# A second load of the second down-projection chunk, and later transposes, in a one-core decoder block

## The chip, the core and the metric

The kernel runs on one core of a Trainium2 chip. A core has five engines with queues of their own: TensorE (PE in the profile: matmuls and transposes; PEld is its loading of weights), VectorE (DVE), ScalarE (ACT), GpSimd (POOL) and SyncE (SP). SP and POOL also issue transfers between the chip's memory and the core's buffer, which 16 DMA engines carry out; those issued by SP show as queue q1 in the profile, those by POOL as q0. The metric is the time of one execution on the device, in microseconds (us). Lower is better.

## The reference

One layer of a decoder block, 512 tokens of 1024 features, in 32-bit floats:

```python
h = rmsnorm(x, pre_mix_norm[l])
proj = h @ w_in[l]                      # queries, keys, values, gates of both mixers
ret = silu(g_r) * retention_chunkwise(q_r, k_r, v_r)
y_r, y_s = ret @ w_ret_out[l], swa @ w_swa_out[l]
merged = sigmoid(gate_r) * y_r + sigmoid(gate_s) * y_s
x = x + rmsnorm(merged @ w_out[l], post_mix_norm[l])
h = rmsnorm(x, pre_mlp_norm[l])
u = jnp.square(jax.nn.relu(h @ w_up[l]))        # 1024 -> 4096
x = x + rmsnorm(u @ w_down[l], post_mlp_norm[l])   # 4096 -> 1024
```

The change concerns the last three lines: the normalised h (h2 in the kernel), the up projection and the down projection.

## The kernel before

**Precision.** Each 32-bit operand is split into a high part, rounded by a copy on ScalarE (`split`, L145), and the low rest, a subtraction on VectorE (L147). A product is three matmuls on TensorE (`mm3`, L190 to L192): high by high, high by low, low by high. whi and wlo are the parts of a weight chunk, left those of the activations. They live in rings: four buffers each for whi and wlo, two for left.

**Fewer products.** Large projections use a Winograd form of the 2 x 2 block product: seven block products instead of eight, with sums of blocks of the weights and of the activations as operands. Sums of weight blocks are made by the transfers: SP loads one block, and POOL issues a second transfer that adds another block into the same buffer (`t_add`, L1296, for w_down; L223 for w_up). Such a transfer is called an add below.

**Up projection.** h2 is transposed on TensorE in two halves of the tokens (`transpose_h2`: four groups of four 128 x 128 transposes into a PSUM bank tin, L1173, each evicted by ScalarE and VectorE). The first NH = 3 blocks of 256 features are computed the plain way by `up_half` (a bank named up, 8 times 3 matmuls of 256 columns), first for the first half of the tokens, so that TensorE has work while the second half is normalised. The transposes of the second half stand after the two blocks fp = 0 and 1, then come the third block and the second half. Blocks 3 to 15 run in Winograd form (`up_pair`, banks named wino); results, squared after relu, go to uc0 to uc3.

**Down projection.** w_down comes in chunks of 1 MB: [128, 4, 512] for a block product and one of four groups j of the 4096 features. tch0 to tch3 hold chunk j of the sum operand T: loaded with block (0, 0), used by p1(j), then an add of block (0, 1) makes the operand of p5(j), two more adds make those of p6(j) and p4(j). The chunks of p2(j) come through raw, a ring of two buffers that is shared with the weight loads of all stages before; rb[j], for p3 and p7, use raw too but for one, which has a buffer of its own. Each product of one j (`product2`) is 24 matmuls of 512 columns, and each needs two halves of whi, of wlo, and one left. The order is

```python
for step, j in ((step_p1, 0), (step_p2, 0), (step_p1, 1), (step_p5, 0), (step_p2, 1),
                (step_p1, 2), (step_p5, 1), (step_p2, 2), (step_p1, 3), (step_p5, 2),
```

tch0 has memory that is free during the up projection. tch1 to tch3 and g_out lie in a pool (dpool3) that takes the memory which the up projection's pools give back, so their loads wait for the last wino matmul that reads from there.

**What sets the order.** A scheduler lays each engine's instructions in one list before the run: by the order of the program, moved ahead by `tc.high_priority(offset)`, held back by `tc.issue_after(ins)`, which places what the block issues on the engine of ins behind ins without a wait for its end, and by what is ready first in its own estimate. At run time each engine takes its list strictly in turn. A transfer is issued when its buffer is free (the last reader of what lay there has finished) and, for an add, when what it adds to has landed and been read.

Of the kernel before, what the change touches and what calls it, by code (L numbers as in the profile page):

```python
# [16 lines left out]
P = 128  # L17
# [14 lines left out]
CHAIN_AHEAD = 400  # L32
SUMS_AHEAD = 0
# [71 lines left out]
def block_kernel(ctx, tc, x, xT, pre_mix, w_in, w_qk, w_v, w_g, w_gate, w_ret, w_swa, w_out, sinks, post_mix,  # L105
                 pre_mlp, w_up, w_down, post_mlp, decay, chunk, dist, out):
    nc = tc.nc
# [8 lines left out]
    def bank(shape, name="ps"):  # L116
        return psum.tile(shape, F32, tag="ps", name=name)
# [23 lines left out]
    last = {}  # L141

    def split(hi, lo, src):

        last["hi"] = nc.scalar.copy(hi, src)  # L145
        last["prior"] = last.get("split")
        last["split"] = nc.vector.tensor_tensor(lo, src, f(hi), op=ALU.subtract)  # L147

    def raw_tile(shape):
        return stream.tile(shape, F32, name="raw", tag="raw", bufs=2)  # L150

    def parts(src, shape):
        hi = stream.tile(shape, F32R, name="whi", tag="whi")
        lo = stream.tile(shape, F32R, name="wlo", tag="wlo")
        split(hi, lo, src)
        return hi, lo
# [30 lines left out]
    def mm3(ps, a, b, first, last, more=False):  # L187

        (ah, al), (bh, bl) = a, b
        nc.tensor.matmul(ps, ah, bh, start=first, stop=False, skip_group_check=more)  # L190
        nc.tensor.matmul(ps, ah, bl, start=False, stop=False, skip_group_check=more)  # L191
        nc.tensor.matmul(ps, al, bh, start=False, stop=last, skip_group_check=more)  # L192

# [1 line left out]
    def wino_pool(stack, side="left"):  # L197
        return stack.enter_context(tc.tile_pool(name="wx", bufs=1, side=side))

    def wino_tokens(wx, b11, b12, b21, b22, f, dst):  # L200

        f11, f12, f21, f22 = f
        nc.vector.tensor_tensor(f11, f11, f12, op=ALU.subtract)
        split(dst[0][:, 0], dst[1][:, 0], f11)
        nc.vector.tensor_tensor(f12, f22, f12, op=ALU.subtract)
        split(dst[0][:, 2], dst[1][:, 2], f12)

        nc.vector.scalar_tensor_tensor(f22, f22, -1.0, f11, op0=ALU.mult, op1=ALU.subtract)
        split(dst[0][:, 1], dst[1][:, 1], f22)
        nc.vector.scalar_tensor_tensor(f21, f22, -1.0, f21, op0=ALU.mult, op1=ALU.subtract)  # L210
        split(dst[0][:, 3], dst[1][:, 3], f21)
        sums = [tuple(d[:, i] for d in dst) for i in range(4)]
        return {"11": b11, "21": b21, "22": b22, "t1": sums[0], "t2": sums[1],
                "t3": sums[2], "t4": sums[3]}
# [50 lines left out]
    def wino_product(ps, a, b, first=True):  # L265
        for k in range(4):
            mm3(
                ps, tuple(o[:, k] for o in a), tuple(o[:, k] for o in b),
                first and k == 0, k == 3, not first,
            )  # L270

    def entry(ps, left, right):

        nc.tensor.matmul(ps, f(left), f(right), start=True, stop=True)
# [106 lines left out]
    for k in range(KD):  # L381
        split(wkv[0][:, k], wkv[1][:, k], raw_kv[:, k])
        split_scaled(xg[0][:, k], xg[1][:, k], xTs[:, k], gT[:, k : k + 1])
        for t in range(NT):
            mm3(kv_ps[t], xcol(k, t), tuple(a[:, k] for a in wkv), k == 0, k == KD - 1)
# [369 lines left out]
    for g in range(SWA_KV):  # L755
        ps = bank([P, SEQ])
# [93 lines left out]
    for h in range(RET_HEADS):  # L850
# [29 lines left out]
        if h == 0:  # L880
# [4 lines left out]
            wx = wino_pool(gctx)  # L885
# [208 lines left out]
    for half in range(2):  # L1094
        zs = [[None, None], [None, None]]
        for n in range(2):
            for t in range(2):
                tt = 2 * half + t
                ps = bank([P, 512])
# [24 lines left out]
    NH = 3  # L1124
# [12 lines left out]
    h2s = [h2spool.tile([P, 4, 4, 256], F32R, name=f"h2s{i}") for i in range(2)]  # L1137
# [3 lines left out]
    wx = wino_pool(uctx)  # L1141
# [4 lines left out]
    quads = [  # L1146
        [tuple(a[:, 0] for a in h2c), tuple(h2b)],
        [tuple(a[:, 1] for a in h2c), tuple(h2d)],
    ]
    h2f = [[uc[3][:, 2 * i + j] for j in range(2)] for i in range(2)]  # L1150

    def up_half(fp, b, w, half):
        both = bank([P, 2, 256], "up")
        ps = both[:, 0]
        if (fp, b, half) == (0, 0, 0):
            entry(both[:, 1, :ENTRY], w[0][:, 0], quads[0][0][0][:, 0, :ENTRY])
        for k in range(KD):
            kw = (k + 4) % KD if b else k
            mm3(
                ps, (w[0][:, kw, :], w[1][:, kw, :]),  # L1160
                tuple(a[:, k % 4] for a in quads[k // 4][half]), k == 0, k == KD - 1,
            )
        dst = uc[fp // 4][:, 2 * b + half, fp % 4]
        nc.scalar.activation(dst, ps, AF.Relu)
        nc.scalar.activation(dst, dst, AF.Square)

    def transpose_h2(half):
        for kp in range(KD // 2):
            ps = bank([P, 2, 256], "tin")
            for k in range(2):  # L1170
                kk = 2 * kp + k
                for t in range(2):
                    nc.tensor.transpose(  # L1173
                        ps[:, k, t * P : (t + 1) * P],
                        h2[2 * half + t][:, kk * P : (kk + 1) * P], ident,
                    )
            i, k0 = kp // 2, 2 * (kp % 2)
            hi, lo = quads[i][half]
            if half and kp == KD // 2 - 1:
                rows = h2[2 * half + 1][:, kk * P : (kk + 1) * P]  # L1180
                entry(bank([P, ENTRY], "entry"), rows, quads[0][0][0][:, 0, :ENTRY])
            split(hi[:, k0 : k0 + 2], lo[:, k0 : k0 + 2], ps)
            nc.scalar.copy(h2f[i][half][:, k0 : k0 + 2], ps)

    held = {}

    def load_up_pair(fp):
        raw = raw_tile([P, 4, 4, P])
        nc.sync.dma_start(raw, w_up[fp])
        return [  # L1190
            parts(raw[:, q : q + 2].rearrange("p q k c -> p (q k) c"), [P, KD, P]) for q in (2, 0)
        ]

    def first_ups(half, fps):
        for fp in fps:
            if half == 0 or fp == 0:
                held[fp] = load_up_pair(fp)
            for b in range(2):
                up_half(fp, b, held[fp][b], half)

    with tc.high_priority(offset=H2_AHEAD):
        transpose_h2(0)
    first_ups(0, range(NH - 1))
    with tc.high_priority(offset=CHAIN_AHEAD):
        transpose_h2(1)
    with tc.high_priority(offset=SUMS_AHEAD):
        h2B = wino_tokens(
            wx, quads[0][0], quads[0][1], quads[1][0], quads[1][1],
            [h2f[0][0], h2f[0][1], h2f[1][0], h2f[1][1]], h2s,
        )  # L1210
    first_ups(0, (NH - 1,))
    first_ups(1, range(NH)[::-1])
    pctx.close()
    tctx.close()
# [5 lines left out]
    tch = [None] * 4  # L1220
# [54 lines left out]
    def left(j, q):  # L1275
        hi, lo = (ring.tile([P, 4, 256], F32R, name=f"left{i}") for i in range(2))
        split(hi, lo, uc[j][:, q])
        return hi, lo

    def right(src):  # L1280
        return [parts(src[:, 2 * i : 2 * i + 2], [P, 2, 512]) for i in range(2)]
# [8 lines left out]
    def product2(ps, j, a, b):  # L1290
        for h in range(2):
            for tb in range(2):
                product(ps, a, b, h, j == 0, j == 3, tb)

    def t_add(dst, k, c, j):
        nc.gpsimd.dma_start(dst, w_down[k, c, j], accum_op=ALU.add)  # L1296

    def load_b(k, c, j, alone=2):
        raw = stream2.tile([P, 4, 512], F32, name="rb") if j == alone else raw_tile([P, 4, 512])
        nc.sync.dma_start(raw, w_down[k, c, j])  # L1300
        return raw
# [8 lines left out]
    p1, p2, p5 = banks2("p1"), banks2("p2"), banks2("p5")  # L1310

    def step_p1(j):
        with tc.high_priority(offset=LEFT_AHEAD if j == 0 else 0):
            with tc.issue_after(last["chain2"].ins):
                b = [parts(tch[j][:, :2], [P, 2, 512])] if j == 0 else right(tch[j])
            with tc.issue_after(last["chain"].ins):
                a = left(j, 0)
            if j == 0:
                with tc.issue_after(last["hi"].ins), tc.issue_after(last["split"].ins):
                    b.append(parts(tch[j][:, 2:], [P, 2, 512]))  # L1320
        t_add(tch[j], 0, 1, j)
        product2(p1, j, a, b)

# [14 lines left out]
    for step, j in ((step_p1, 0), (step_p2, 0), (step_p1, 1), (step_p5, 0), (step_p2, 1),  # L1338
                    (step_p1, 2), (step_p5, 1), (step_p2, 2), (step_p1, 3), (step_p5, 2),
                    (step_p2, 3), (step_p5, 3)):  # L1340
        step(j)
# [85 lines left out]
    for j in range(2):  # L1427
        a, b = left(j, 3), right(tch[j])
# [21 lines left out]
    for i in range(2):  # L1450
        c = slice(i * 256, (i + 1) * 256)
        ps = bank([P, 256], "p4c")
# [53 lines left out]
```

## Time and profile before

| | |
|---|---|
| runs | 718.5, 718.7, 720.9 us; median 718.7 |
| profiled execution | 718.92 us, span of its profile 717.1 us, granted TensorE clock 0.997 |
| TensorE matmul busy | 705.3 us, 98% of the span |
| VectorE, ScalarE, GpSimd busy | 539.3, 430.7, 61.3 us |
| bytes moved by transfers | 119.37 MB, mean 166 GB/s |

Times in rows are counted from the start of the span. A timeline row gives start, duration, engine, line, operation, the tile written and those read, and in brackets the idle time just before it with what ended it. A waits row gives the waiting engine and line, what it waited for, the us in total, the times, and the longest. A row on transfers gives the tiles, the issuing queue, the size, and the us from issue to landing. A busy TensorE share is of pipelined matmuls: each lasts longer than the distance to the next one.

### The profile page before, as it was taken

The numbers are of one execution on the slowest core, as the hardware profiler recorded it, in microseconds if no ns is written. First come the engines' busy times: TensorE is split into PE (matmuls) and PEld (weight loads), VectorE is DVE, ScalarE is ACT, GpSimd is POOL, SyncE is SP. The second block draws the span as 40 slices with busy tenths as digits, with TensorE's granted clock in tenths as the row PEclk, the third lists the DMA queues.
The fourth block names the chain that finished last, engine by engine and source line by source line (L and its number), as shares of the span: only waits on it lengthen the run. The fifth ranks groups of instructions, "written<-read, shape, count | busy, mean of one in ns | idle before, by whom it ended". The sixth has DMA issues, their size and how long they took to land.

```text
span 717.1 us, 11473 instructions
## 1 busy us (share of the span) xinstructions
PE 705.3 (98%) x4528; PEld 630.1 (88%) x4528; DVE 539.3 (75%) x816; ACT 430.7 (60%) x733; POOL 61.3 (9%) x77
## 2 busy tenths in 40 slices
PE   9999999999999999999999999999999999999996
PEld 8877879898788999989888999999999788888885
DVE  5699988685985767566945866778777688977797
ACT  6657667566665525435733866766668566655561
POOL 0200100121100000000011100000000110010010
PEclk9999999999999999999999999999999999999998
DMA  9964623966444455553661619876753999698603
GB/s 316 333 176 89 151 60 102 266 154 139 89 148 117 129 137 147 156 168 101 218 258 69 162 45 283 205 192 158 212 144 118 315 273 237 148 207 198 117 1 117
DMA packets 40613, 119.37 MB, mean 166 GB/s; under 512 B 3568, under 2 KB 17008, under 8 KB 34416
## 3 DMA queue, kind: packets, MB, share of 16 engines
q1 hardware_dynamic: 33504, 81.28, 32.4%
q0 software_dynamic: 6768, 37.23, 27.8%
q8 instruction: 35, 0.57, 0.3%
q14 instruction: 18, 0.15, 0.1%
q10 hardware_dynamic: 288, 0.14, 0.1%
HBM read 116.54 MB, written 2.10 MB: 165 GB/s over the span
## 4 chain that ended last, share of the span: by engine, by line
PE 76%; DVE 9%; DMA 7%; ACT 5%; issue 2%; POOL 1%; POOLq 0%; SPq 0%; DVEq 0%; ACTq 0%
PE wino L190 9%; PE wino L192 9%; PE wino L191 9%; PE p L191 5%; PE p L190 5%; PE p L192 5%; DVE wlo L147 3%; DMA raw<-in_w_in 3%; PE yr L192 2%; PE yr L190 2%; PE ps L190 2%; PE ps L192 2%; PE yr L191 2%; PE ps L191 2%; ACT whi L145 2%
## 5 line engine op out<-in xcount | busy, mean ns | idle before, releaser
L147 DVE TENSOR_TENSOR wlo<-raw,whi 128x1024 fp32r<-128x1024 f32 (+1 forms) x80 | 96.3, 1208 | 41.2 <-ACT whi L145 41.1
L145 ACT CAST whi<-raw 128x1024 fp32r<-128x1024 f32 (+1 forms) x80 | 82.9, 1042 | 32.6 <-DMA raw<-in_w_in 7.2
L191 PE MATMUL p<-wlo,left 128*128 128x512 f32 x216 | 84.2, 390 | 0.8 <-DVE wlo L147 0.8
L190 PE MATMUL p<-whi,left 128*128 128x512 f32 x216 | 84.1, 390 | 0.6 <-ACT whi L145 0.6
L192 PE MATMUL p<-whi,left 128*128 128x512 f32 x216 | 84.0, 390 | 0.0
L190 PEld LDWEIGHTS p<-whi,left 128*128 128x128 f32 x216 | 40.5, 188 | 9.7 <-ACT whi L145 1.0
L191 PEld LDWEIGHTS p<-wlo,left 128*128 128x128 f32 x216 | 40.5, 188 | 9.5 <-DVE wlo L147 1.1
L192 PEld LDWEIGHTS p<-whi,left 128*128 128x128 f32 x216 | 40.5, 188 | 8.7 <-DVE left L147 0.4
L147 DVE TENSOR_TENSOR wlo<-tch,whi 128x1024 fp32r<-128x1024 f32 x32 | 38.7, 1219 | 9.2 <-ACT whi L145 9.2
L145 ACT CAST p<-rs 128x1024 fp32r<-128x1024 f32 x22 | 23.1, 1052 | 36.5 <-DVE rs L244 36.4
L145 ACT CAST left<-uc 128x1024 fp32r<-128x1024 f32 x28 | 29.4, 1052 | 23.1 <-PE p L191 19.8
L147 DVE TENSOR_TENSOR left<-uc,left 128x1024 fp32r<-128x1024 f32 x28 | 34.1, 1220 | 10.2 <-ACT left L145 10.2
L145 ACT CAST whi<-tch 128x1024 fp32r<-128x1024 f32 x32 | 33.3, 1049 | 13.6 <-PE p L192 6.5
L147 DVE TENSOR_TENSOR p<-rs,p 128x1024 fp32r<-128x1024 f32 x22 | 27.0, 1226 | 16.7 <-ACT p L145 16.7
L147 DVE TENSOR_TENSOR wlo<-rs,whi 128x1024 fp32r<-128x1024 f32 x23 | 28.1, 1224 | 15.1 <-ACT whi L145 12.5
L190 PE MATMUL wino<-h2s,p 128*128 128x256 f32 x104 | 28.8, 277 | 0.0
L192 PE MATMUL wino<-h2s,p 128*128 128x256 f32 x104 | 28.7, 276 | 0.0
L191 PE MATMUL wino<-h2s,p 128*128 128x256 f32 x104 | 28.7, 276 | 0.0
L190 PE MATMUL wino<-h2c,whi 128*128 128x256 f32 x104 | 28.7, 276 | 0.0
L191 PE MATMUL wino<-h2c,whi 128*128 128x256 f32 x104 | 28.7, 276 | 0.0
L192 PE MATMUL wino<-h2c,wlo 128*128 128x256 f32 x104 | 28.7, 276 | 0.0
L190 PE MATMUL wino<-h2s,whi 128*128 128x256 f32 x104 | 28.7, 276 | 0.0
(411 smaller groups left out, 2352.2 us busy)
## 6 DMA issues: line engine op xcount, KB each, us to landing
tch<-in_w_down POOLq DMA_DIRECT2D x12, 1024.0 KB, 9.2
raw<-in_w_down SPq DMA_DIRECT2D x7, 1024.0 KB, 7.8
rs<-in_w_up SPq DMA_DIRECT2D x13, 512.0 KB, 4.5
rs<-in_w_up POOLq DMA_DIRECT2D x13, 512.0 KB, 5.6
raw<-in_w_up SPq DMA_DIRECT2D x13, 512.0 KB, 5.4
acc<-in_w_v POOLq DMA_DIRECT2D x4, 1024.0 KB, 9.0
rs<-in_w_gate SPq DMA_DIRECT2D x8, 512.0 KB, 4.1
acc<-in_w_g POOLq DMA_DIRECT2D x4, 1024.0 KB, 8.0
```

The lines of the kernel that those rows point to most:

```text
L145: last["hi"] = nc.scalar.copy(hi, src)
L147: last["split"] = nc.vector.tensor_tensor(lo, src, f(hi), op=ALU.subtract)
L190: nc.tensor.matmul(ps, ah, bh, start=first, stop=False, skip_group_check=more)
L191: nc.tensor.matmul(ps, ah, bl, start=False, stop=False, skip_group_check=more)
L192: nc.tensor.matmul(ps, al, bh, start=False, stop=last, skip_group_check=more)
```

## The change

It has two parts. In the first, `step_p1(1)` no longer reads tch1 but a second copy of the same chunk, loaded into a raw buffer (`load_b(0, 0, 1, 4)`); tch1 is loaded as before and serves from the add for p5(1) on. In the second, `transpose_h2(1)` and the sums behind it are issued from within `up_half` of the block fp = 1, b = 1: behind the sixth of its 24 matmuls (k = 1), by `tc.issue_after`. mm3 returns its last matmul for that.

```diff
-    def up_half(fp, b, w, half):
+    def up_half(fp, b, w, half, amid=None):
...
-            mm3(
+            done = mm3(
                 ps, (w[0][:, kw, :], w[1][:, kw, :]),
                 tuple(a[:, k % 4] for a in quads[k // 4][half]), k == 0, k == KD - 1,
             )
+            if amid and k == 1:
+                amid(done.ins)
...
-                up_half(fp, b, held[fp][b], half)
+                up_half(fp, b, held[fp][b], half, amid if b and fp == NH - 2 else None)
...
-    first_ups(0, range(NH - 1))
-    with tc.high_priority(offset=CHAIN_AHEAD):
-        transpose_h2(1)
-    with tc.high_priority(offset=SUMS_AHEAD):
-        h2B = wino_tokens(
-            wx, quads[0][0], quads[0][1], quads[1][0], quads[1][1],
-            [h2f[0][0], h2f[0][1], h2f[1][0], h2f[1][1]], h2s,
-        )
+    h2B = {}
+
+    def second_half(ins):
+        with tc.high_priority(offset=CHAIN_AHEAD), tc.issue_after(ins):
+            transpose_h2(1)
+        with tc.high_priority(offset=SUMS_AHEAD):
+            h2B.update(wino_tokens(
+                wx, quads[0][0], quads[0][1], quads[1][0], quads[1][1],
+                [h2f[0][0], h2f[0][1], h2f[1][0], h2f[1][1]], h2s,
+            ))
+
+    first_ups(0, range(NH - 1), second_half)
...
     def step_p1(j):
+        src = load_b(0, 0, j, 4) if j == 1 else tch[j]
         with tc.high_priority(offset=LEFT_AHEAD if j == 0 else 0):
             with tc.issue_after(last["chain2"].ins):
-                b = [parts(tch[j][:, :2], [P, 2, 512])] if j == 0 else right(tch[j])
+                b = [parts(src[:, :2], [P, 2, 512])] if j == 0 else right(src)
```

SP's list around the start of the down projection, before. raw_6240 is for p2(0), raw_6354 for p2(1), raw_6468 for p2(2); rb_6871 is for p3(2).

```order
L1300 DMA raw_6240<-in_w_down 128x2048
L1300 DMA raw_6354<-in_w_down 128x2048
L1225 DMA tch1_6166<-in_w_down 128x2048
L1225 DMA tch2_6168<-in_w_down 128x2048
L1225 DMA tch3_6170<-in_w_down 128x2048
L1267 DMA g_out_6172<-in_post_mlp_norm 128x1024
L1300 DMA raw_6468<-in_w_down 128x2048
L1300 DMA rb_6871<-in_w_down 128x2048
```

And with the change, where raw_6274 is the second copy for p1(1), raw_6356 is for p2(1) and raw_6470 for p2(2):

```order
L1306 DMA raw_6240<-in_w_down 128x2048
L1306 DMA raw_6274<-in_w_down 128x2048
L1231 DMA tch1_6166<-in_w_down 128x2048
L1231 DMA tch2_6168<-in_w_down 128x2048
L1231 DMA tch3_6170<-in_w_down 128x2048
L1273 DMA g_out_6172<-in_post_mlp_norm 128x1024
L1306 DMA raw_6356<-in_w_down 128x2048
L1306 DMA raw_6470<-in_w_down 128x2048
L1306 DMA rb_6873<-in_w_down 128x2048
```

The copy for p1(1) took the second place, and the load for p2(1) moved from there to behind the three tch loads and g_out.

POOL's list of adds, before, with the semaphores that each waits for (DVE: an instruction of VectorE; DMAHW: a load issued by SP; DMASW: an add; PE: a matmul):

```order
L1296 DMA tch0_4566<-in_w_down 128x2048 [waits DVE_49]
L1296 DMA tch1_6166<-in_w_down 128x2048 [waits DMAHW6_49,DVE_49]
L1296 DMA tch0_4566<-in_w_down 128x2048 [waits DMASW7_49,DVE_49]
L1296 DMA tch2_6168<-in_w_down 128x2048 [waits DMAHW7_49,DVE_49]
L1296 DMA tch1_6166<-in_w_down 128x2048 [waits DMASW0_49,DVE_49]
```

With the change:

```order
L1302 DMA tch0_4566<-in_w_down 128x2048 [waits DVE_49]
L1302 DMA tch1_6166<-in_w_down 128x2048 [waits DMAHW6_49,PE_49]
L1302 DMA tch0_4566<-in_w_down 128x2048 [waits DMASW7_49,DVE_49]
L1302 DMA tch2_6168<-in_w_down 128x2048 [waits DMAHW7_49,DVE_49]
L1302 DMA tch1_6166<-in_w_down 128x2048 [waits DMASW0_49,DVE_49]
```

The first add into tch1 no longer waits for VectorE, which read tch1 for p1(1), but for the load into tch1 and for the matmul that the load into tch1 itself waits for, the last wino matmul on that memory.

TensorE's list at the transposes of the second half, as the difference (with its sign) between the two:

```order
 L190 MATMUL up<-h2c_4095,whi 128x256
-L1173 MATMUL tin<-ident,zg 128x128 x16
+L191 MATMUL up<-h2c_4096,whi 128x256
+L192 MATMUL up<-h2c_4095,wlo 128x256
+L190 MATMUL up<-h2c_4095,whi 128x256
+L191 MATMUL up<-h2c_4096,whi 128x256
+L192 MATMUL up<-h2c_4095,wlo 128x256
+L1175 MATMUL tin<-ident,zg 128x128 x16
 L274 MATMUL entry<-h2c_4095,zg 128x32
```

The sixteen transposes moved behind five matmuls of the block fp = 1 that stood after them; the one ahead of them was there before. All other matmuls keep their places.

More of the change, by code (lines that the diff above doesn't have):

```diff
@@ L191, in mm3 @@
         nc.tensor.matmul(ps, ah, bl, start=False, stop=False, skip_group_check=more)
-        nc.tensor.matmul(ps, al, bh, start=False, stop=last, skip_group_check=more)
+        return nc.tensor.matmul(ps, al, bh, start=False, stop=last, skip_group_check=more)
     def wino_pool(stack, side="left"):
@@ L1192, in load_up_pair, with first_ups @@
         ]
-    def first_ups(half, fps):
+    def first_ups(half, fps, amid=None):
         for fp in fps:
@@ L1319, in step_p1 @@
                 with tc.issue_after(last["hi"].ins), tc.issue_after(last["split"].ins):
-                    b.append(parts(tch[j][:, 2:], [P, 2, 512]))
+                    b.append(parts(src[:, 2:], [P, 2, 512]))
         t_add(tch[j], 0, 1, j)
```

## The prediction

> **What bounds the kernel now.** I read the page first, for the engine that is full.
>
> ```profile
> span 717.1 us, 11473 instructions
> PE 705.3 (98%) x4528; PEld 630.1 (88%) x4528; DVE 539.3 (75%) x816; ACT 430.7 (60%) x733; POOL 61.3 (9%) x77
> ```
>
> TensorE is busy 98% of the span. An edit that leaves its matmuls alone can win only the time in which TensorE stands, and every new stand is a loss. The view of waits, for TensorE alone, gives the stands (us in total, times, longest); three of its rows belong to this change:
>
> ```profile
> PE p L191 <- DVE wlo L147: 0.8, 1, 0.8
> PE p L190 <- ACT whi L145: 0.6, 1, 0.6
> PE tin L1173 <- ACT uc L1164: 0.3, 1, 0.3
> ```
>
> The chain of waits says what lies behind the first two (start, us, what):
>
> ```profile
> 556.21 0.36 PE wino L190
> 557.87 7.80 DMA tch<-in_w_down
> 565.69 1.06 ACT whi L145
> 566.77 1.24 DVE wlo L147
> 568.05 0.51 PE p L191
> ```
>
> The load of the second chunk into tch1 cannot be issued before the last wino matmul, since tch1 lies in memory that the up projection gives back. It lands at 565.69, 2.36 us of cast and subtraction follow, and p1(1), the first product with that chunk, has been waiting. TensorE's own rows there (timeline):
>
> ```profile
> 565.85 0.39 PE L192 MATMUL p<-whi,left 128*128 128x512 f32 x1
> 566.79 0.50 PE L190 MATMUL p<-whi,left 128*128 128x512 f32 x1 [0.56 <-ACT whi L145]
> 568.05 0.51 PE L191 MATMUL p<-wlo,left 128*128 128x512 f32 x1 [0.76 <-DVE wlo L147]
> 568.40 0.39 PE L192 MATMUL p<-whi,left 128*128 128x512 f32 x1
> ...
> 578.82 0.39 PE L190 MATMUL p<-whi,left 128*128 128x512 f32 x1
> ```
>
> In an undisturbed stretch these matmuls start every 0.227 us (568.40 to 578.82 is 46 of them). The two late starts cost 0.94 - 0.23 = 0.71 and 1.26 - 0.23 = 1.03: **1.75 us**. The row at 578.82 is the first matmul of p2(1), two products of 24 matmuls later; its second stands at 579.05.
>
> **The transposes.** They stand once:
>
> ```profile
> 404.33 0.27 PE L1173 MATMUL tin<-ident,zg 128*128 128x128 f32 x1
> 404.88 1.83 PE L1173 MATMUL tin<-ident,zg 128*128 128x128 f32 x15 [0.28 <-ACT uc L1164]
> ```
>
> Fifteen take 1.83, 0.12 each, so the second is 0.43 late. Five up matmuls, counted in the order's rows as those now ahead, fill that hole with work that had to be done anyway. I take **-0.4 us**; below it 0 (the wait moves along with its group), above it 0.43. The evictions behind the transposes come some 0.2 us later and feed products much further on.
>
> **The extra load.** Nothing is taken away on any engine: the casts and subtractions of p1(1) read another buffer. One 1 MB load is added to SP's queue. It takes the raw buffer and the place in the queue that the load for p2(1) had:
>
> ```profile
> 538.63 9.48 SPq L1300 DMA_DIRECT2D raw<-in_w_down  x2
> 557.87 1.96 SPq L1225 DMA_DIRECT2D tch<-in_w_down  x3
> 559.87 0.56 SPq L1267 DMA_DIRECT2D g_out<-in_post_mlp_norm  x1
> 560.53 0.44 SPq L1300 DMA_DIRECT2D raw<-in_w_down  x1
> 561.01 0.51 SPq L1300 DMA_DIRECT2D rb<-in_w_down  x1
> ```
>
> The second of the pair in the first row was issued at 547.8 and, by the view of transfers for that moment, landed 6.2 us later, at 554.0:
>
> ```profile
> raw<-in_w_down SPq DMA_DIRECT2D x1, 1024.0 KB, 6.2
> ```
>
> So p1(1)'s data is there 12 us before TensorE wants it. On VectorE its two subtractions come ahead of the operand left of uc1, which now starts here:
>
> ```profile
> 562.03 1.22 DVE L147 TENSOR_TENSOR left<-uc,left 128x1024 fp32r<-128x1024 f32 x1
> ```
>
> One of the two fits in VectorE's idle time before, one pushes this row to about 563.3 + 1.2 = 564.5 at its end; p1(1) can begin at 565.85 + 0.23 - 0.4 = 565.7. The wait at p1(1) is gone: **-1.75 us**, by a margin of one subtraction.
>
> **What is late next.** Without stands p2(1) begins 48 matmuls after 565.7, at 576.55, its second matmul at 576.8. The second needs its load landed 2.36 us earlier, by 574.4. But that load is now the one issued at 560.5, behind three chunks and g_out, where the load for p2(2) stood. That one took
>
> ```profile
> raw<-in_w_down SPq DMA_DIRECT2D x1, 1024.0 KB, 15.3
> ```
>
> and landed at 575.8. Even with that, moved up by 0.4 to 575.4, p2(1)'s second matmul comes at 577.8 and 1.0 us of the 2.15 is given back. It gets worse, since the add into tch1 moves too. GpSimd issued it here, when the casts of p1(1) had read tch1, and the next add behind it:
>
> ```profile
> 569.54 0.86 POOL L1296 DMA_DIRECT2D tch<-in_w_down  x1 [13.43 <-DVE wlo L147]
> 572.94 0.89 POOL L1296 DMA_DIRECT2D tch<-in_w_down  x1 [2.54 <-DVE wlo L147]
> ```
>
> No cast reads tch1 any more, and in the order its wait on VectorE has become one on TensorE, on the wino matmul that was over before tch1's load began. It goes as soon as that load lands: 565.3 + 0.3 = 565.6, **3.9 us earlier**, and from its first packet it takes bandwidth from the load that is now urgent. Three stretches show how much (view of transfers by queue: packets, MB, share of 16 engines): 564 to 570, loads alone; 574 to 584, loads and adds; 570.2 to 574, up to the first add packets.
>
> ```profile
> q1 hardware_dynamic: 359, 2.53, 99.8%
> ...
> q0 software_dynamic: 190, 1.43, 68.6%
> q1 hardware_dynamic: 187, 1.28, 32.0%
> ...
> q1 hardware_dynamic: 238, 1.41, 105.8%
> ```
>
> Alone the loads move 2.53 / 6 = 0.42 MB a us; beside adds 1.28 / 10 = **0.128**, since the queues take turns packet by packet (190 to 187) and an add's packet holds an engine for twice as long. How long after its issue an add gets its first packet, with a long queue of loads ahead, two places show. From 569.54 to 573.8, and in the retention stage from the issue below at 128.78 to 133, only loads moved; in the next microsecond, 133 to 134, both did:
>
> ```profile
> 128.78 0.87 POOL L223 DMA_DIRECT2D rs<-in_w_qk  x1 [50.06 <-PE ret_v L192]
> ```
>
> ```profile
> q1 hardware_dynamic: 289, 1.58, 102.6%
> ...
> q1 hardware_dynamic: 250, 1.61, 99.6%
> ...
> q0 software_dynamic: 22, 0.09, 56.6%
> q1 hardware_dynamic: 31, 0.13, 46.3%
> ```
>
> Both times about 4.3 us, in which 1.6 MB of loads went by. So the first add packet comes at 565.6 + 4.3 = 569.9, which is 570.3 on the old clock. There p2(1)'s load and what is ahead of it still lack the 1.41 MB of the row above. At 0.128 that is 11.0 us: bytes through at 580.9. Landing came 1.8 us after the bytes in the old place (574.0 to 575.8); I take 1.1, so **582**. Both adds hold out that long: 2.1 MB at 0.143 a us is 14.7 us. p2(1)'s second matmul is at 584.35 instead of 579.05: **+5.3 us**, in which the 1.75 and the 0.4 are already swallowed. Bounds of the landing: 575.4 (the add never gets ahead) and 584.5 (it gets its turn at once, worked out below). Later loads have room: p2(2)'s follows 8 us behind and is wanted 16 us after p2(1).
>
> **The clock.** TensorE would stand from 576.55 to about 583, 6.5 us. How the granted clock takes that, only the end of the span shows, where the last matmul ends at 710.5 (window, five engines, PEclk, DMA share, GB/s):
>
> ```profile
> 710.00:711.00 1.00, 0.48 (x5) 0.28 (x3) 0.79 (x3) 0.51 (x2) 0.00 (x0) 1.00 0.88 328
> 712.00:713.00 1.00, 0.00 (x0) 0.00 (x0) 0.56 (x2) 0.00 (x0) 0.67 (x1) 0.86 0.00 0
> 713.00:714.00 1.00, 0.00 (x0) 0.00 (x0) 1.00 (x2) 0.00 (x0) 0.00 (x0) 0.50 0.00 0
> ```
>
> It falls to half 2.2 us after the last matmul. How long it stays low under new work is not shown. Nothing lost is one bound; the 4.3 us for which it lies at half up to the span's end, at half speed, are 2.15 us, the other. I take as long as the fall took, 2.2 us at half: **+1.2 us**. The Trainium skill ("TensorE: Matmul & The Clock Gate", Part 1) has the clock come back after a busy window of about 3.4 us, by which the loss would be 1.7 and the sum 0.5 higher; its idle window of 3.4 us is longer than the 2.2 of this trace.
>
> **Sum.** The profiled execution took 718.92 for a span of 717.1; the median of the runs is 718.7, so I work from that. 5.3 + 1.2 = +6.5, **725.2 us**. This case by itself reaches from a landing at 579.5 with no loss of clock (+2.8) to one at 583.5 with 2.15 (+9): 721.5 to 727.7.
>
> **Rivals.** *The load slips through.* If the add waits until the loads ahead have gone, however early it is issued, p2(1)'s load lands at 575.4 and the change wins 2.15 - 1.0, some 1.2: 717.5. For it: at 573.8 the first add packet came just as the load's bytes were through. Against it: 133 to 134 shows loads still moving beside the add, and both places fit one amount of 1.6 MB. It decides if the first add packet comes after 574. Chance 0.20.
>
> *Part of it.* The add starts 2 to 3 us later than I say, or hurts less: landing 577 to 579.5, +0.3 to +2.8, little clock: 720.2. Chance 0.13.
>
> *The add takes its turn at once,* at the end of its issue, 566.5. The load then lacks 1.41 + 3.3 x 0.42 = 2.8 MB; in the 14.7 us of the two adds 1.88 go, the rest at 0.42: 583.4, landed 584.5, +7.8 and 1.2: 727.7. The rows speak against it, twice 4.3 us. Chance 0.08. This is what the Trainium skill's rule would give ("DMA: Bandwidth & Descriptors", Queues, rings and completion order): each engine goes round the queues that have work, a packet at a time. The trace agrees once both run (190 packets to 187), not in the first 4 us.
>
> *All is won* (716.5): the change doing just what it says, with p2(1) unhurt. The load would have to land by 574.4, and the old place never did better than 575.8. Chance 0.03.
>
> **Chances and range.** The forecast has 0.56. What this kernel's measurement can tell from no change is about 0.5%, 3.6 us. Slower by more: the forecast but for its lowest part, and the add at once, 0.60. Within: the load slipping through, part of it, all won, the lowest part, 0.38. Faster by more than 3.6 us no mechanism reaches, 0.02 for what I have not seen. The range takes in the load that slips through below and the add at once above: 717.3 to 728.
>
> **What would show it.** The profile after should show no stand at p1(1); an add into tch1 issued near 565.6; a load of p2(1) issued near 560.5 and landing 20 us later; one stand of about 6 to 7 us at p2(1), waiting for whi and that load; and a granted clock below 1.00 just behind it. I am wrong if the first add packets come after 574, or if p2(1) begins before 578.

## The result, and the profile after

The changed kernel takes **728.14 us** (median of six executions, 727.32 to 730.73) against 719.61 us for the kernel before, measured beside it: ratio 1.0119, 95% interval 1.0084 to 1.0153. It is slower by some 8.5 us. The forecast said 725.2 with a range up to 728.0, so the sign was right and the size was not.

The profiled execution took 730.73 us. Its page begins:

```profile
span 729.0 us, 11473 instructions
...
PE 708.5 (97%) x4528; PEld 632.6 (87%) x4528; DVE 539.7 (74%) x816; ACT 430.7 (59%) x733; POOL 61.5 (8%) x77
```

The instructions are the same in number. TensorE is busy 3.2 us longer with the same matmuls, and stands some 9 us longer. The view of TensorE's waits says where (engine and line, what it waited for, us in total, times, longest):

```profile
PE p L190 <- ACT whi L145: 8.8, 1, 8.8
...
PE p L191 <- DVE wlo L147: 0.5, 1, 0.5
```

There is no row for tin any more: the transposes do not stand. The two small waits of p1(1) are gone too; what is left under the same two names is one place, p2(1). The chain of waits around it (start, us, what):

```profile
557.88 0.37 PE wino L190
559.50 0.24 PE p L192
559.91 0.49 SPq L1231
...
560.99 0.51 SPq L1273
561.60 24.84 DMA raw<-in_w_down
586.46 1.05 ACT whi L145
587.53 1.24 DVE wlo L147
588.81 0.80 PE p L191
589.61 0.43 PE p L192
...
592.17 0.32 PE p L192
592.48 0.23 PE p L190
```

It is one story. The last wino matmul frees the memory, SyncE (SPq) issues the three tch loads and g_out, then p2(1)'s load, which takes 24.8 us. A cast and a subtraction follow, p2(1) starts, and its matmuls come 0.43 us apart until 592.2, 0.23 us from there on. GpSimd's adds, in the timeline:

```profile
568.08 0.86 POOL L1302 DMA_DIRECT2D tch<-in_w_down  x1 [10.29 <-PE p L192]
571.57 0.89 POOL L1302 DMA_DIRECT2D tch<-in_w_down  x1 [2.62 <-DVE wlo L147]
```

The first add into tch1 is issued 8.55 us after tch1's load (559.53); before, it was 569.54 - 557.87 = 11.67. From 574 to 582 loads and adds shared the transfer engines as follows (view of transfers by queue: packets, MB, share of 16 engines); the third and fourth rows are 568.0 to 572.6, the fifth is the load queue from 559.5 to 583.2, the last from 559.5 to 586.4:

```profile
q0 software_dynamic: 161, 1.19, 71.5%
q1 hardware_dynamic: 159, 1.04, 32.5%
...
q1 hardware_dynamic: 271, 1.74, 97.1%
q0 software_dynamic: 2, 0.02, 1.7%
...
q1 hardware_dynamic: 715, 4.74, 50.1%
...
q1 hardware_dynamic: 771, 5.14, 47.8%
```

Loads move 1.04 / 8 = 0.13 MB a us beside adds, and up to 572.6, 4.5 us after the issue of the first add into tch1, they had the engines almost to themselves. Three tch chunks, g_out and p2(1)'s load are 4.72 MB; the queue has moved that much at 583.2. But p2(1)'s load lands at 586.4, by when the queue has moved 0.4 MB more, of loads behind it.

The clock, in windows of one us (five engines, PEclk, transfer share, GB/s):

```profile
581.00:582.00 1.00, 0.00 (x0) 0.00 (x0) 0.00 (x0) 0.00 (x0) 0.00 (x0) 0.99 0.95 262
...
587.00:588.00 1.00, 0.45 (x1) 0.29 (x1) 0.47 (x1) 1.00 (x2) 0.00 (x0) 0.50 0.98 369
...
592.00:593.00 1.00, 1.00 (x5) 0.84 (x4) 1.00 (x2) 0.00 (x0) 0.00 (x0) 0.89 1.02 434
...
725.00:726.00 1.00, 0.00 (x0) 0.00 (x0) 0.56 (x1) 0.00 (x0) 0.00 (x0) 0.67 0.23 88
```

A mean of 0.99 over one us is 0.02 us at half, one of 0.89 is 0.22 us. So the clock falls to half at 581.98 and comes back at 592.22; the last row, from the end of the span, is for later. p2(1) starts at 587.55, but its first matmul loses nothing by the half clock: the second waits for VectorE's subtraction and comes 1.26 us later, as it did at p1(1) before with the clock whole (566.79 to 568.05). From the second, at 588.81, to 592.22 the matmuls run at half speed: 3.41 us, so 1.7 us lost.

**Where the 8.5 us are.** Counted from the issue of tch1's load, so that what lies ahead in the two executions drops out, p2(1)'s second matmul stood at 579.05 - 557.87 = 21.18 before and stands at 588.81 - 559.53 = 29.28 now: +8.1. The last matmul (timeline, before and now) is

```profile
710.20 0.28 PE L192 MATMUL p4c<-whi,left 128*128 128x256 f32 x1
...
721.58 0.28 PE L192 MATMUL p4c<-whi,left 128*128 128x256 f32 x1
```

From the second matmul of p2(1) to there it was 131.15 and is 132.77: +1.6, the clock. From there to the end of the span it was 6.9 and is 7.4: +0.5. The last output transfer is issued 4.0 us after the last matmul in both (714.20 and 725.59), so this lies behind it. All profiled kernels with the second copy have 7.4 there, the one with the transposes alone has 7.0; why, no run shows. That makes 10.2 of the 11.9 us by which the span is longer. The other 1.7 lie ahead of tch1's load, the gain by the transposes among them, and the windows there show a half clock that is no part of the change:

```profile
72.00:73.00 1.00, 1.00 (x4) 0.56 (x3) 0.88 (x1) 1.00 (x2) 0.00 (x0) 0.50 1.00 383
```

It lasted from 69.97 to 73.39 with TensorE at work throughout, so it cost up to 1.7 us. In the profile of the kernel before the clock was whole there, and so it was in that of g_out last (below), which is the changed kernel up to tch1's load.

### The profile page after: what moved, and what is told of

It is laid out like the page before. It is cut to its first block, busy times and chain, and to the rows that moved or that the text cites. A ratio compares the mean times of both kernels' runs of the same rounds, so it can differ in the third digit from the quotient of the medians.

```text
span 729.0 us, 11473 instructions
## 1 busy us (share of the span) xinstructions
PE 708.5 (97%) x4528; PEld 632.6 (87%) x4528; DVE 539.7 (74%) x816; ACT 430.7 (59%) x733; POOL 61.5 (8%) x77
## 4 chain that ended last, share of the span: by engine, by line
PE 72%; DMA 9%; DVE 9%; ACT 6%; issue 2%; POOL 1%; SPq 0%; POOLq 0%; DVEq 0%; ACTq 0%
PE wino L190 9%; PE wino L192 9%; PE wino L191 9%; DMA raw<-in_w_down 4%; PE p L191 4%; PE p L192 4%; PE p L190 4%; DVE wlo L147 3%; DMA raw<-in_w_in 3%; ACT whi L145 2%; PE yr L191 2%; PE ps L191 2%; PE yr L190 2%; PE ps L192 2%; PE ps L190 2%
## 5 line engine op out<-in xcount | busy, mean ns | idle before, releaser
L147 DVE TENSOR_TENSOR wlo<-raw,whi 128x1024 fp32r<-128x1024 f32 (+1 forms) x82 | 98.7, 1209 | 55.4 <-ACT whi L145 55.3
L145 ACT CAST whi<-raw 128x1024 fp32r<-128x1024 f32 (+1 forms) x82 | 84.9, 1042 | 45.0 <-DMA raw<-in_w_down 19.1
L147 DVE TENSOR_TENSOR wlo<-tch,whi 128x1024 fp32r<-128x1024 f32 x30 | 36.4, 1218 | 5.5 <-ACT whi L145 5.5
L147 DVE TENSOR_TENSOR p<-rs,p 128x1024 fp32r<-128x1024 f32 x22 | 27.0, 1225 | 16.7 <-ACT p L145 16.7
L145 ACT CAST whi<-tch 128x1024 fp32r<-128x1024 f32 x30 | 31.4, 1050 | 10.0 <-PE p L192 8.0
```

## The experiments

The theory: the second copy pushes p2(1)'s load behind 3.7 MB of other loads, and the first add into tch1, now early, takes bandwidth while that load is still on its way; the stand that follows also costs clock. The rivals: the transposes do it; the place in the queue alone does it, the add nothing; the clock costs nothing in the end.

### The transposes alone

```diff
-        src = load_b(0, 0, j, 4) if j == 1 else tch[j]
+        src = tch[j]
```

> The second part of the change alone: the transposes five matmuls later, p1(1) reads tch1 as before. Theory A (all of the loss comes from the transfers): the second transpose no longer stands, 0.4 us faster than before, 718.3 beside 718.7, and the two late starts at p1(1) stay (0.71 and 1.03 us). Theory C (the sums and the parts of the second half, which now come later on ScalarE, cost something at the first wino products): 0 to 2 us slower.

Measured: 718.35 us, ratio 0.9983 [0.9969, 0.9997]. The row for tin is gone, and p1(1) stands as before:

```profile
PE p L191 <- DVE wlo L147: 0.8, 1, 0.8
...
PE p L190 <- ACT whi L145: 0.7, 1, 0.7
```

So this part wins a little, 0.2 to 2.2 us by the interval, and the whole loss is the other part's.

### The second copy alone

The changed kernel with `transpose_h2(1)` and its sums back behind `first_ups(0, range(NH - 1))`, as in the kernel before.

> The first part alone: the second copy for p1(1), transposes as before. Theory A: the whole loss stands here, 8.5 to 9.5 us slower than before, with the load of p2(1) landing 24 to 25 us after its issue and TensorE standing about 9 us at p2(1). Theory C: less than 8 us.

Measured: 728.48 us, ratio 1.0113 [1.0087, 1.0139], the time of the whole change. Its stand is the same, and the row for tin is back with 0.3 us:

```profile
PE p L190 <- ACT whi L145: 8.7, 1, 8.7
```

### The add held back

The first add into tch1 goes behind the second add into tch0 on GpSimd's list, so it is issued some 13 us after tch1's load instead of 8.55.

```diff
-        t_add(tch[j], 0, 1, j)
+        if j != 1:
+            t_add(tch[j], 0, 1, j)
...
-            t_add(tch[j], 1, 1, j)
+            second = t_add(tch[j], 1, 1, j)
+        if j == 0:
+            with tc.issue_after(second.ins):
+                t_add(tch[1], 0, 1, 1)
```

> The whole change, but the first add into tch1 stands behind the second add into tch0 in GpSimd's list, so that no add is issued before about 571 us instead of 568.1 with the change. Nothing else moves. Theory A (the add that was issued too early takes the bandwidth from the load of p2(1)): first add packet near 575.5, the load of p2(1) lands 15 to 17 us after its issue, TensorE stands 1 to 2.5 us at p2(1), and the time is between 1.2 us faster and 1 us slower than before, 717.5 to 719.7. Theory B (the place behind three chunks and g_out is what costs, whatever the adds do): the load still takes over 20 us and the time stays over 725.

Measured: 723.04 us, ratio 1.0055 [1.0034, 1.0075]. ScalarE's casts and TensorE's late matmuls, from the timeline:

```profile
576.15 1.99 ACT L145 CAST whi<-raw 128x1024 fp32r<-128x1024 f32 x2 [4.55 <-DMA raw<-in_w_down]
...
589.22 1.04 ACT L145 CAST whi<-tch 128x1024 fp32r<-128x1024 f32 x1 [8.22 <-DMA tch<-in_w_down]
```

```profile
577.25 0.50 PE L190 MATMUL p<-whi,left 128*128 128x512 f32 x1 [1.08 <-ACT whi L145]
578.51 0.50 PE L191 MATMUL p<-wlo,left 128*128 128x512 f32 x1 [0.76 <-DVE wlo L147]
...
591.27 0.51 PE L190 MATMUL p<-whi,left 128*128 128x512 f32 x1 [1.81 <-ACT left L145]
592.72 0.50 PE L192 MATMUL p<-whi,left 128*128 128x512 f32 x1 [0.64 <-DVE left L147]
```

p2(1)'s load, issued at 559.46 in the same place of the queue, lands at 576.15: 16.7 us after issue. With the early add it took 24.8, and in three more profiles 24.2 (the second copy alone), 24.6 (the stand filled, below) and 22.8 (the change again). So 6 to 8 us are the add's doing, and the rival "the place alone" falls. The time I had given for this kernel was missed, since I had not followed the add itself: it lands at 589.2, and p5(1), which reads it, stands instead. The transfers are short at this place as a whole, and the delay of one shows up in the other.

### The load ahead

p2(1)'s load is issued right behind tch1's, ahead of tch2, tch3 and g_out.

```diff
+    early = {}
+    for k, j in ((1, 0), (0, 1), (1, 1)):
+        early[k, j] = raw_tile([P, 4, 512])
+        nc.sync.dma_start(early[k, j], w_down[k, 0, j])
     for j in range(1, 4):
         load_t(j)
```

> The whole change, but the load of p2(1) is issued right behind the one for tch1, ahead of tch2, tch3 and g_out, which each go one place back; the add into tch1 goes out as early as with the change. Theory A: the load of p2(1) lands before 571, so the early add can no longer hurt it; no stand at p1(1) nor at p2(1), 2.1 us faster than before, 716.6; the load of p2(2) becomes the next one to be late, wanted near 590 and landing near 588, so up to 2 us of that may be given back. Theory B: the same 716.6. If the early add hurts whichever load comes next, p2(2) takes the stand: slower than before by 3 us or more.

Measured: 721.05 us (718.61 to 725.05), ratio 1.0020 [0.9999, 1.0041]. p1(1) and p2(1) do not stand. p2(2) does, in the profiled execution:

```profile
595.30 0.50 PE L192 MATMUL p<-whi,left 128*128 128x512 f32 x1 [1.48 <-DVE left L147]
```

Its load, issued at 563.42 behind g_out, landed 27.2 us later, at 590.6 (view of transfers); the wait bears the name of the last step behind that landing:

```profile
raw<-in_w_down SPq DMA_DIRECT2D x1, 1024.0 KB, 27.2
```

So the place in the queue settles p2(1), and most of the 8.5 us is back; but the shortage moves on to p2(2)'s load. The times spread over 6 us, and one profile does not tell what the longer ones add.

### g_out last

The load of g_out, 0.5 MB, moves from ahead of p2(1)'s load to the end of the first phase.

```diff
-    nc.sync.dma_start(g_out, post_mlp.to_broadcast([P, D_MODEL]))
...
+    with tc.issue_after(last["load"].ins):
+        nc.sync.dma_start(g_out, post_mlp.to_broadcast([P, D_MODEL]))
```

> The whole change, with only the 0.5 MB load of g_out moved from ahead of p2(1)'s load to much later. Theory A with the rate of 0.128 MB a us beside adds: 0.52 MB less ahead is 4.1 us, so p2(1)'s load takes 20.7 us instead of 24.8 and the stand shrinks from 9 to 5 us; the time falls by 4 us, a little more if the clock stays up, to 723.5 to 724.5. If the load's time is set by the adds (it can land only when both are through), it stays at 24 to 25 us and the time at 728.

Measured: 722.88 us (719.55 to 724.06), ratio 1.0043 [1.0028, 1.0058]; the profiled execution took 720.11. There p2(1)'s load, issued at 558.87, landed after 18.2 us:

```profile
577.04 1.99 ACT L145 CAST whi<-raw 128x1024 fp32r<-128x1024 f32 x2 [5.55 <-DMA raw<-in_w_down]
...
578.13 0.49 PE L190 MATMUL p<-whi,left 128*128 128x512 f32 x1 [2.07 <-ACT whi L145]
```

At 0.13 MB a us, 0.52 MB less ahead is worth 4 us; against the 22.8 to 24.8 us of the four profiles above it was 4.6 to 6.6 here, and 5.3 us of the time by the medians. The mean granted clock goes with the time: 0.997 in the executions of 719.6 to 720.6 us, 0.993 to 0.994 in those of 723.2 to 724.1, as if the clock fell in these and not in the profiled one. That is argued from means; no profile of a longer execution was taken.

### The stand filled

35 multiplications of the 128 x 128 identity by itself, read by nobody, stand on TensorE's list between p5(0) and p2(1). It was run twice, the second time beside the changed kernel itself.

```diff
+    def fill(n):
+        ps = bank([P, P], "fill")
+        for _ in range(n):
+            nc.tensor.matmul(ps, ident, ident, start=True, stop=True)
...
         step(j)
+        if (step, j) == (step_p5, 0):
+            fill(35)
```

> The whole change, with 35 transposes-sized matmuls of the identity (0.23 us each, 8.1 us, into a free bank that nobody reads) between p5(0) and p2(1), so that TensorE is busy while the load of p2(1) is awaited. It computes nothing that is used. Clock theory (the profile of the change lost 2.1 us behind the stand because the granted clock was at half from 582 to 592.9): the stand lasts as long, the clock stays at 1.00, and the time is 2 us lower than the change's, 726. If the clock costs nothing: 728, or more if the filling outlasts the stand.

> The changed kernel with the stand at p2(1) filled by 35 matmuls whose result is read by nobody, once more, beside the changed kernel itself in the same call. If the half clock behind the stand costs what the windows say, 2.1 us, and the filled kernel loses 0.6 of it again in a late stand of its own, its median lies 1.5 us under that of the changed kernel. If the clock costs nothing in the end, or the fill costs as much as it saves, the two medians lie within 0.5 us.

> The changed kernel as it is, for the comparison with the filled stand in the same call: 728.1 again, a stand of 8 to 9 us at p2(1), and the clock at half for about 4 us behind it.

Measured: 727.82 us (726.11 to 734.31), ratio 1.0138 [1.0100, 1.0175]; the second time 727.49 (726.48 to 736.19), 1.0132 [1.0094, 1.0170], beside 729.67 (729.47 to 730.06), 1.0138 [1.0119, 1.0158], for the changed kernel, whose profile this time has a stand of 7.2 us at p2(1), not the 8 to 9 I had expected, and a half clock at 70 us again. In the profile of the first, the fill (each multiplication in two records) lasted 7.97 us by the timeline,

```profile
575.96 7.97 PE L1348 MATMUL fill<-ident 128*128 128x128 f32 x70
...
585.21 0.50 PE L190 MATMUL p<-whi,left 128*128 128x512 f32 x1 [1.27 <-ACT whi L145]
```

and by the windows the clock stayed whole (the 1.00 ahead of the last two numbers):

```profile
580.00:584.00 4.00, 3.94 (x36) 3.75 (x34) 0.00 (x0) 0.00 (x0) 0.00 (x0) 1.00 1.03 291
```

Its span is 726.1 against 729.0 and 728.3, though it has a late stand of 0.7 us of its own (at 690.3) and no half clock at 70 us as the other two have. By the medians it is 0.3 us under the changed kernel across calls and 2.2 within one, and the intervals of the ratios overlap: what the clock costs cannot be read from these times. It can from the traces of three executions that had the stand: the change, the second copy alone, and the change again. The second of these starts p2(1) earlier than the first (timeline):

```profile
586.24 0.79 PE L190 MATMUL p<-whi,left 128*128 128x512 f32 x1 [8.75 <-ACT whi L145]
587.50 0.79 PE L191 MATMUL p<-wlo,left 128*128 128x512 f32 x1 [0.47 <-DVE wlo L147]
```

Its clock, in windows of one us:

```profile
582.00:583.00 1.00, 0.00 (x0) 0.00 (x0) 0.00 (x0) 0.00 (x0) 0.00 (x0) 0.56 0.95 262
...
592.00:593.00 1.00, 1.00 (x5) 0.81 (x4) 0.00 (x0) 0.44 (x1) 0.61 (x1) 0.82 0.68 287
```

The third starts it earlier still (timeline):

```profile
585.87 0.80 PE L190 MATMUL p<-whi,left 128*128 128x512 f32 x1 [7.23 <-ACT whi L145]
587.13 0.80 PE L191 MATMUL p<-wlo,left 128*128 128x512 f32 x1 [0.47 <-DVE wlo L147]
```

And its clock:

```profile
582.00:583.00 1.00, 0.00 (x0) 0.00 (x0) 0.00 (x0) 0.00 (x0) 0.00 (x0) 0.59 0.98 262
...
592.00:593.00 1.00, 1.00 (x5) 0.81 (x4) 0.00 (x0) 0.77 (x1) 0.87 (x1) 0.79 0.97 410
```

Worked out as above, half clock lasts from 582.12 to 592.36 and from 582.18 to 592.42. In all three it is 10.24 us, and it ends at 592.2 to 592.4 whether work resumed at 587.55, 586.24 or 585.87. From the second matmul to that end there are 3.41, 4.86 and 5.29 us, and the matmuls lose half of them: 1.7, 2.4 and 2.6 us. The time from p2(1)'s second matmul to the last one agrees: 131.15 before and 131.55 with g_out last, both with the clock whole, against 132.8, 133.6 and 133.8 in these three. So the rival that the clock costs nothing falls by the traces, not by the medians.

The Trainium skill ("TensorE: Matmul & The Clock Gate", Part 1) has the clock judged in windows of 3.413 us that run freely, whatever the kernel does. The traces agree: 10.24 is three of them, the first empty, the second cut by the restart, the third full. And the next fall in the change's own profile, at 725.34 by the row shown above for the end of the span, comes 133.12 us after the return, 39 of them. The edges of the windows are not tied to the start of the span: in the kernel before one lies at 712.72, by the fall at its end, and so, 39 windows earlier, at 579.60, where the three stands have one at 578.6 to 578.8. That the three agree to 0.2 us is chance as far as these traces show, and in another execution the clock may return at another moment.

### The urgent loads first

The list of SyncE in the order in which TensorE wants the data: p2(0), the copy for p1(1), tch1, p2(1), tch2, p2(2), tch3, g_out.

```diff
-    for j in range(1, 4):
-        load_t(j)
...
+    early, prior = {}, None
+    for k, j in ((1, 0), (0, 1), ("t", 1), (1, 1), ("t", 2), (1, 2), ("t", 3), ("g", 0)):
+        with tc.issue_after(prior.ins) if prior else ExitStack():
+            if k == "t":
+                prior = load_t(j)
...
+            else:
+                early[k, j] = raw_tile([P, 4, 512])
+                prior = nc.sync.dma_start(early[k, j], w_down[k, 0, j])
```

> The whole change, with SP's loads in the order in which TensorE wants them: p2(0), copy for p1(1), tch1, p2(1), tch2, p2(2), tch3, g_out, then as before. Theory A (a load is late only if bytes wanted later stand ahead of it when the adds begin): p2(1) lands near 568, tch2 near 571, p2(2) near 580 where 590 is wanted, tch3 near 589 where 596 is wanted; no stand from p1(1) to p2(2); 716.5, that is 2.1 us faster than 718.7 (ratio 0.997). Theory D (the added megabyte makes something late whatever the order): not faster than before.

Measured: 718.28 us, ratio 0.9990 [0.9977, 1.0003]: the loss is gone, and a gain is not shown. In the first phase TensorE does not stand; just behind it, it does once:

```profile
621.51 0.50 PE L191 MATMUL p<-wlo,left 128*128 128x512 f32 x1 [1.25 <-DVE wlo L147]
```

An add issued at 596.5 took 13.2 us by the view of transfers for 596 to 598. My reading is that what ScalarE and VectorE had to do behind it piled up; the next run tries it.

```profile
tch<-in_w_down POOLq DMA_DIRECT2D x1, 1024.0 KB, 13.2
```

### And rb later

The kernel of the last section, with the load of rb for p3(2) (1 MB, issued at 574.97 there) held back to behind rb for p3(1).

```diff
-        nc.sync.dma_start(raw, w_down[k, c, j])
+        with tc.issue_after(loaded["rb"].ins) if (k, j) == (1, alone) and c else ExitStack():
+            loaded["rb" if c else "p2"] = nc.sync.dma_start(raw, w_down[k, c, j])
```

> As the kernel with the urgent loads first, and the load of rb for p3(2), 1 MB, held back on SyncE's list from ahead of rb for p3(0) to behind rb for p3(1) (it is wanted only some 75 us after its old issue). Theory: what is left of the loss there (a stand of 1.25 us at 621.5, behind an add issued at 596.5 that took 13 us) is a shortage of transfers between 575 and 605, where the transfer engines are busy all the time; 1 MB less there lands that add 2 us earlier or more, the stand goes, and the span is 715.3 instead of 716.7: 1.9 us under the kernel before, ratio 0.997. Rival: the stand comes from the order of VectorE's instructions (seven others ahead of that subtraction), then it stays and the ratio with it, 0.999.

Measured: **717.07 us** against 719.25 beside it, ratio 0.9966 [0.9942, 0.9990], the best of all. No row for p is left among TensorE's waits, and the page begins:

```profile
span 715.1 us, 11475 instructions
...
PE 704.8 (99%) x4528; PEld 630.4 (88%) x4528; DVE 539.6 (75%) x816; ACT 430.6 (60%) x733; POOL 61.3 (9%) x77
```

The late add takes 10.2 us instead of 13.2 (view of transfers for 596 to 598: tiles, queue, size, us to landing):

```profile
tch<-in_w_down POOLq DMA_DIRECT2D x1, 1024.0 KB, 10.2
```

rb is issued at 607.59 (timeline).

So the stand was a shortage of transfers, not the order of VectorE's work, and the change as a whole does win when the extra megabyte is paid for: by sending what is urgent first and what is not urgent later. How much of this 0.3% is the second copy's is not shown by the times, since the transposes alone gave 0.0 to 0.3%; by the profiles the span is 715.1 here and 716.5 with the transposes alone.

## Why the prediction was right or wrong

**What bounds the kernel: right.** TensorE's full queue, one stand as the loss, no work added to it.

**p1(1) and the transposes: right.** Both stands are gone. The transposes alone gave between 0.2 and 2.2 us, where I had 0.4.

**What is late next: right, with its mechanism.** I had p2(1)'s load issued near 560.5 (561.6 in an execution that is 1.7 us late there), an early add into tch1 (8.55 us after tch1's issue; I had 565.6 - 557.5 = 8.1), its first packet 4.3 us after issue (about 4.5), loads at 0.128 MB a us beside adds (0.13), and the load's bytes through 23.4 us after tch1's issue (583.2 - 559.53 = 23.7). Holding the add back moved the landing by 6 to 8 us and taking g_out away by 4.6 to 6.6: both causes are shown by runs.

**The landing: mis-sized.** I let it follow the bytes by 1.1 us, against the one row I had, 1.8. It was 3.2 us in this execution (586.4 less 583.2). By the same count, total bytes of the queue against landing, it was 2.9 for the second copy alone, 2.0 for the change again, 2.4 with the add held back, 1.4 without g_out. My value lies under all of them. While it waits, the queue moves 0.4 MB of later loads, so it seems that some of the 16 engines were through while another was not; which one, and why, the views do not tell. With 0.3 for the bytes this makes p2(1) 2.4 us later than forecast (29.28 against 584.35 - 557.47 = 26.88).

**The clock: mis-sized, and of the wrong form.** I took 2.2 us at half behind the restart, +1.2, with 2.15 as the upper bound. The runs show half clock up to the edge of a window, 592.2 to 592.4, so the loss is half of the distance from the second matmul to there: 1.7 us in this execution, and 2.4 and 2.6, above my bound, in the two others with the stand. It also couples the two terms: in the change again p2(1)'s second matmul came 1.5 us earlier after tch1's issue (587.13 - 559.39 = 27.74 against 29.28) and lost 0.9 us more to the clock. So part of what the late landing cost would have gone to the clock had it been early; how much, no run at the forecast moment shows. The sentence of the Trainium skill ("TensorE: Matmul & The Clock Gate", Part 1) that I weighed, with a loss of 1.7, gives the size of this execution, where the second matmul happened to stand on the edge of a window (581.98 + 2 x 3.413 = 588.81), and not that of the two others.

**The end of the span: left out.** Behind the last output's issue 0.5 us more passed than before. I had no term for it, and its cause stays open.

**The sum.** Forecast 5.3 + 1.2 = 6.5. By the trace the same terms are 8.1 - 0.4 = 7.7 (the 5.3 had the transposes in it) and 1.6, with 0.5 at the end 9.8: the landing makes 2.4 of the missing 3.3, the clock 0.4, the end 0.5. By the medians it is 8.5 against 719.6 and, against 719.25, 10.4 when it was run again, with the half clock at 70 us in that profile. The range's top, 728.0, rested on the add taking its turn at once, with the same small landing lag and clock; it left out that these two could be wrong in the forecast case itself.

**The rivals.** "The load slips through" and "all is won" fall with the landing at 586. "Part of it" falls likewise. "The add takes its turn at once" comes nearest in time and is wrong in mechanism: 4.5 us passed between the add's issue and the stretch in which both queues moved.

## What to carry to other kernels

A load is not free because a buffer is: ask which load it pushes back in the queue, how many megabytes are then ahead of it, and whether a transfer that the edit releases early will share the engines with it. Where a queue is full, send what is wanted first first, and hold back what is wanted late; here that turned +1.2% into -0.3%. When TensorE stands long enough for the clock to fall, count the loss from the first matmul that does not wait for data anyway up to the moment at which the clock returns, not as a fixed time behind the restart.

## What the runs showed of the hardware that I had not expected

- Half clock lasted 10.24 us three times over, and work that resumed at 587.55, 586.24 or 585.87 did not shift its end. In the last of these, by the windows, TensorE had matmuls in 2.67 of the 3.41 us from 585.59 to 589.00, and the clock did not come back at 589.00.
- The fall came 3.2 us after the last matmul in the change (578.8 to 581.98), 4.6 and 3.5 us in the two other profiles with the stand, and 2.2 us at the end of the span of the kernel before. The half clock at 69.97 followed a stretch of 3.41 us in which TensorE was busy for 2.50.
- With adds and loads in both queues, a 1 MB load landed 1.4 to 3.2 us after its queue had moved all bytes up to its end.
- Under a 4 MB load queue an add got its first packets some 4.5 us after its issue, as in the two places of the kernel before, and from then on adds took seven tenths of the engines' time. With no load in the queue the add into tch0, issued at 556.91, had its first packets 1.6 us after.
